# Half of the up projection with seven products per block instead of three eighths, and one of its weight sums formed by DMA

## The chip, the cores and the metric

The kernel runs on one core of one Trainium2 chip. What is measured is the device time of one launch in microseconds. Three timed runs of the kernel before gave 1578.73 to 1579.29 us, median 1578.91 us.

## The reference

One layer of an encoder: a retention branch and an attention branch, merged by gates, then an MLP with a squared ReLU. Batch 1, 256 tokens, width 2048, hidden width 8192, float32. Only the MLP matters for this change; `z` is what is tiled differently.

```python
def reference(x, positions, ...):
    h = x
    for l in range(DEPTH):
        u = _rmsnorm(h, norm_mix_g[l])
        h = h + _mixer(u, positions, ...)
        z = _rmsnorm(h, norm_mlp_g[l]) @ w_up[l]          # (256 x 2048) @ (2048 x 8192)
        h = h + jnp.square(jax.nn.relu(z)) @ w_down[l]    # (256 x 8192) @ (8192 x 2048)
    return _rmsnorm(h, norm_f_g)
```

## The kernel before

**Numbers as pairs.** Each float32 matrix is split in two parts, `hi` (rounded by ACT, line 550 in `split`, or 168) and `lo` (the rest, subtracted by DVE, line 551 or 169), and a product is formed as hi\*hi + hi\*lo + lo\*hi. So every weight tile is loaded by SP, cast by ACT, subtracted by DVE, and then used by PE.

**Two ways through the up projection.** The 8192 columns are cut into two kinds of work.

- A *unit* (class `Unit`) makes 128 columns for all 256 tokens. It has two parts, one for each half of the 16 blocks of depth; a part loads 512 KB (line 1225), splits it, and runs eight matmuls of 512 columns (line 176, hidden state hi and lo side by side) and eight of 256 columns (line 180). At its end ACT copies the sum out (1246), DVE adds the two halves (1247), ACT applies ReLU and square (1250, 1211), and POOL stores 128 KB of the hidden state to DRAM (1212).
- A *step* (class `Step`) multiplies 256 rows of depth by 1024 columns as 2x2 blocks with seven products in place of eight. A *group* is eight steps (j = 0 to 7), which accumulate seven PSUM tiles `zs`, one for each product; it makes 1024 columns, as many as eight units. A step has four parts: 0 (two products, from the loaded blocks `ra`), 1 (two, from the sum `fa`), 2 (two, from the sum `fb`), 3 (one, from the first block of `rb`). Each product is three matmuls of 512 columns (333 to 335).

Before the change three groups (`SU = 3`) make 3072 columns and 40 units the other 5120.

**A step's weights.** SP loads `ra` (two blocks, 512 KB, tile `sraw`, two buffers, line 300) and `rb` (two blocks, 512 KB, tile `raw`, five buffers which are shared with the units, line 301). DVE forms `fa` = `ra` + the second block of `rb` (line 307), and then `fb` = `fa` + blocks of `ra` and `rb` in two additions (316, 317). `fa` and `fb` lie in the tile `forms`, four slots used in turn, so those of a step are used again two steps later. `ra`, `fa`, `fb` and the first block of `rb` are then split, in that order, one for each part.

**End of a group.** When the last step of a group has run, `s_end` combines the seven PSUM tiles: four ACT copies (522 to 528) of products 3, 5, 1 and 7, and DVE additions (520), of which the first reads product 6, the second product 2, the third product 4. The seven tiles take all four banks of the pool `pmm` (products 3, 4, 2, 5) and three of the four of `pat` (6, 1, 7). The next group's tiles go into the same banks. A unit needs one bank of `pat`, and so does a *turn*: four transposes (1264) of the group's result, ReLU and square, and a store of 256 KB. Each group's four turns are spread over the steps 1 and later of the next.

**Order.** The order on ACT, DVE, PE, SP and POOL in the MLP is the program's own, written by `stream`: at part n it first issues the loads up to part n + 6, then the casts and subtractions up to part n + 4, then the matmuls of part n and, if that ends a unit, its copy out, then what is due later. There are seven pairs of buffers for `hi` and `lo` (four, and three named `more`). The list `parts` begins with three units (`EARLY`), then has the steps with units between them, then two units (`LATE`), and then the down projection, whose steps (`Seven`, a subclass of `Step`, and `Eight`) use the same loads and sums from `w_down`. Units are put after part 3 of every step but the last, and after part 1 of every second step.

Of the kernel before, what the change touches and what calls it, by code (L numbers as in the profile page):

```python
# [17 lines left out]
ALU = mybir.AluOpType  # L18

P = 128  # L20
# [7 lines left out]
CHUNK = 64  # L28
DFF = 8192
FT = DFF // P  # L30
SU = 3
SJ = KT // 2
ST = SU * 1024 // P
EARLY, LATE = 3, 2
AHEAD = 4
PAIRED = 6
MAKE = 7, 2 * EARLY + 18
SUMS = (4, 7, 10), (0, 1, 2)
MANUAL = {getattr(mybir.EngineType, n) for n in ('Activation', 'DVE', 'PE', 'SP', 'Pool')}
# [66 lines left out]
def block_kernel(ctx: ExitStack, tc: tile.TileContext, A):  # L106
    nc = tc.nc
    V, SC, G, PE = nc.vector, nc.scalar, nc.gpsimd, nc.tensor
# [7 lines left out]
    def big(name, dt=F32, shape=(P, KT, S)):  # L116
        return act.tile(list(shape), dt, tag="act16", name=name)

    class Pair:
        def __init__(self, name):  # L120
            self.t = [big(f"{name}{i}", F32R, (P, KT // 2, 2, S)) for i in range(2)]
# [35 lines left out]
    def wtile(kind, shape):  # L157
        uid[0] += 1
        dt, bufs = (F32, 5) if kind == "raw" else (F32R, 4)
        return wp.tile(shape, dt, tag=kind, bufs=bufs, name=f"{kind}{uid[0]}")  # L160

    def weights(src, shape, into=None):
        raw = wtile("raw", shape)
        hi, lo = into or (wtile(kind, shape) for kind in ("hi", "lo"))
        load = nc.sync.dma_start(raw, src)
        if uid[0] < 40:
            tc.keep_in_program_order(load)
        SC.copy(hi, raw)  # L168
        V.tensor_tensor(out=lo, in0=raw, in1=hi.bitcast(F32), op=ALU.subtract)  # L169
        return hi, lo  # L170
# [102 lines left out]
    def pair(shape):  # L273
        pool, more = env["pool"], env["more"]
        slot[0] += 1
        if slot[0] % (4 + more) < 4:
            return [wtile(kind, shape) for kind in ("hi", "lo")]
        if env["big"]:
            t = env["big"][:, slot[0] % (4 + more) - 4]
            n = math.prod(shape[1:])  # L280
            return [t[:, i, :n].rearrange("p (a b) -> p a b", a=shape[1]) for i in range(2)]
        return [
            pool.tile(shape, F32R, tag=f"more{kind}", bufs=more, name=f"more{kind}{uid[0]}_{slot[0]}")
            for kind in ("hi", "lo")
        ]

    class Step:
        def __init__(self, qs, src, x, j, between, end):
            self.qs, self.src, self.x, self.j, self.between, self.end = qs, src, x, j, between, end
            self.ws = {}  # L290

        def load(self, part):
            if part:
                return
            self.rb = wtile("raw", [P, 2, 512])
            if env["sraw"]:
                self.ra = env["pool"].tile([P, 2, 512], F32, tag="sraw", bufs=2, name=f"sraw{uid[0]}")
            else:
                self.ra = wtile("raw", [P, 2, 512])
            nc.sync.dma_start(self.ra, self.src[:, :2])  # L300
            nc.sync.dma_start(self.rb, self.src[:, 2:])
            forms = env["forms"]
            self.fa, self.fb = (forms[:, (2 * self.j + i) % forms.shape[1]] for i in range(2))

        def prep(self, part):
            if part == 0:
                V.tensor_tensor(  # L307
                    out=self.fa, in0=self.rb[:, 1:].to_broadcast([P, 2, 512]), in1=self.ra, op=ALU.add
                )
                self.middle()  # L310
            r = (self.ra, self.fa, self.fb, self.rb[:, :1])[part]
            hi, lo = pair([P, r.shape[1], 512])
            split(hi, lo, r)
            self.ws[part] = hi, lo
            if part == 0:
                V.tensor_tensor(out=self.fb[:, 0], in0=self.fa[:, 0], in1=self.ra[:, 1], op=ALU.add)
                V.tensor_tensor(out=self.fb[:, 1], in0=self.fb[:, 0], in1=self.rb[:, 0], op=ALU.add)
# [97 lines left out]
            pass  # L415

    class Seven(Step):
        def __init__(self, banks, src, h, n, end=None):
            super().__init__(None, src, None, n, None, end)
            self.banks, self.h = banks, h  # L420
# [127 lines left out]
    def split(hi, lo, val, scale=None):  # L548
        if scale is None:
            SC.copy(hi, val)  # L550
            V.tensor_tensor(out=lo, in0=val, in1=hi.bitcast(F32), op=ALU.subtract)  # L551
        else:
            SC.activation(hi, val, AF.Copy, scale=scale)
            V.scalar_tensor_tensor(
                lo, in0=val, scalar=scale, in1=hi.bitcast(F32), op0=ALU.mult, op1=ALU.subtract
            )
# [44 lines left out]
    for k in range(KT):  # L601
        t = lead0[:, N_VEC:] if k == 0 else wtile("raw", [P, LEAD])
# [654 lines left out]
    def turn(u, jj):  # L1257
        pT = atps(f"zt{u}{jj}")
        for j in range(2):
            kt = 2 * jj + j  # L1260
            for t in range(2):
                o = j * S + t * P
                src = zo[:, 0, 2 * t + kt // 4, kt % 4 * P : kt % 4 * P + P]
                PE.transpose(pT[:, o : o + P], src, ident)
        square(4 * u + jj, pT)

    def step(u, j, qs):
        def end():
            sums = s_end(qs, zo[:, 0].rearrange("p (t c) n -> p t c n", t=2), zo[:, 1])
            next(sums)  # L1270
            later.extend([d, lambda: next(sums)] for d in SUMS[u == SU - 1])
            turns.extend(lambda jj=jj: turn(u, jj) for jj in range(4))
# [13 lines left out]
    early = [Unit(i, 0) for i in range(EARLY)]  # L1286
    parts = [(e, h) for h in range(2) for e in early]
    units = list(range(EARLY, FT - ST - LATE))
    slots = [(u, j, h) for u in range(SU) for j in range(SJ) for h in (1, 3)][:-1]
    whole = [t for t in slots if t[2] == 3]  # L1290
    room = len(units) - len(whole)
    halves = [t for t in slots if t[2] == 1]
    if room >= 0:
        use = set(whole) | {halves[i * len(halves) // room] for i in range(room)}
    else:
        use = {t for t in whole if t[1] != PAIRED or t[0] >= -room}
    for u in range(SU):
        qs = {}
        for j in range(SJ):
# [69 lines left out]
    def finish(half, t, c, n, lo=0, hi=512):  # L1369
        h = residual(half, t, c)[:, lo:hi]  # L1370
        ps = both[half].q[ROLE[t, c]][:, lo:hi]
        V.scalar_tensor_tensor(h, in0=ps, scalar=rh2[:, t : t + 1], in1=h, op0=ALU.mult, op1=ALU.add)

        def square():
            SC.activation(ps, h, AF.Square, accum_out=ssf[:, t, n : n + 1])

        return square
# [90 lines left out]
    with tc.manual_schedule(engines=MANUAL):  # L1468
        stream(parts, after)
        assert not later  # L1470
        for t in range(2):
            for c in range(2):
# [10 lines left out]
                else:  # L1483
                    halves = [finish(1, t, 1, 3, 0, 256)]
# [86 lines left out]
```

## Time and profile before

| what | value |
|---|---|
| timed runs, median (lowest to highest) | 1578.91 us (1578.73 to 1579.29) |
| profiled execution, span from first to last instruction | 1577.3 us |
| mean granted TensorE clock | 0.998 |
| first product of the first step to the last of the last group | 907.9 to 1221.95 us |
| the second and the third group with its units | 107.05 us each |
| DMA in 905 to 1222 us | 69.80 MB, mean 220 GB/s |
| busy in the span: PE, DVE, ACT | 99%, 83%, 61% |

The profiled execution is described by its span; the median of the timed runs stands 1.6 us above it. PE's busy time is made of matmul records that overlap (a matmul of 512 columns has a record of 390 ns, and the next one begins some 0.23 us after it), so work on PE is read here from the starts of instructions, not from the sum of their durations. PEld is the loading of PE's weights, one in front of each matmul; its starts follow one another in the same rhythm. A row of the timeline that stands for several like instructions ends in x and their count.

### The profile page before, as it was taken

How to read it: one execution, taken by the hardware profiler on the slowest of the kernel's cores; microseconds unless marked ns; L12 is line 12 of the kernel's file. 1: busy time of each engine (PE TensorE's matmuls, PEld its weight loads, DVE VectorE, ACT ScalarE, POOL GpSimd, SP SyncE). 2: the span in 40 equal slices, each digit the busy share in tenths (PEclk: the TensorE clock that was granted, in tenths of full speed). 3: DMA queues.
4: the chain of work that ended last, by engine and by line, in shares of the span. 5: the costliest groups of instructions: out<-in, count | busy, mean ns of one | idle time of the engine just before them, and what ended most of it. 6: DMA issues, size and time to landing. Idle time of an engine off the chain costs nothing.

```text
span 1577.3 us, 21401 instructions
## 1 busy us (share of the span) xinstructions
PE 1565.2 (99%) x7671; PEld 1317.0 (84%) x7671; DVE 1313.6 (83%) x1780; ACT 959.0 (61%) x1405; POOL 38.9 (2%) x75
## 2 busy tenths in 40 slices
PE   9999999999999999999999999999999999999997
PEld 7888888888898888888888888888888888888886
DVE  7898877899967988875667689887978899989996
ACT  6545655566545667765445566676766766666664
POOL 0000000000000000000000000010000100000000
PEclk9999999999999999999999999999999999999999
DMA  8666655466656564443565666667675977786873
GB/s 322 212 197 205 231 164 161 157 203 208 204 178 222 190 203 142 136 135 132 188 214 186 240 221 226 218 209 236 203 246 196 366 267 244 241 308 216 267 254 114
DMA packets 107626, 333.70 MB, mean 212 GB/s; under 512 B 11264, under 2 KB 12160, under 8 KB 106496
## 3 DMA queue, kind: packets, MB, share of 16 engines
q1 hardware_dynamic: 104208, 318.71, 60.5%
q0 software_dynamic: 3168, 11.54, 1.8%
q10 hardware_dynamic: 144, 2.10, 0.4%
q8 instruction: 60, 0.98, 0.3%
q14 instruction: 46, 0.38, 0.1%
HBM read 319.72 MB, written 12.58 MB: 211 GB/s over the span
## 4 chain that ended last, share of the span: by engine, by line
PE 81%; issue 0%; DVE 0%; ACT 0%; DVEq 0%; POOLq 0%; POOL 0%; ACTq 0%
PE z L176 9%; PE dn L357 7%; PE dn L359 7%; PE dn L358 7%; PE z L180 5%; PE zs L333 2%; PE zs L334 2%; PE zs L335 2%; PE lt L199 2%; PE mo L214 2%; PE mo L217 2%; PE mo L215 2%; PE wo L214 2%; PE wo L215 2%; PE wo L217 2%; PE gm L357 2%
## 5 line engine op out<-in xcount | busy, mean ns | idle before, releaser
L169 DVE TENSOR_TENSOR lo<-raw,hi 128x1024 fp32r<-128x1024 f32 (+1 forms) x148 | 173.2, 1172 | 97.2 <-ACT hi L168 97.0
L551 DVE TENSOR_TENSOR lo<-raw,hi 128x1024 fp32r<-128x1024 f32 (+3 forms) x214 | 232.3, 1102 | 22.9 <-ACT hi L550 22.5
L168 ACT CAST hi<-raw 128x1024 fp32r<-128x1024 f32 (+1 forms) x148 | 149.4, 1011 | 166.2 <-PE mo L215 46.2
L550 ACT CAST hi<-raw 128x1024 fp32r<-128x1024 f32 (+3 forms) x214 | 200.1, 954 | 55.5 <-issue 7.8
L551 DVE TENSOR_TENSOR morelo<-raw,morehi 128x1024 fp32r<-128x1024 f32 (+1 forms) x118 | 127.2, 1099 | 19.6 <-ACT morehi L550 19.1
L550 ACT CAST morehi<-raw 128x1024 fp32r<-128x1024 f32 (+1 forms) x118 | 109.1, 950 | 12.6 <-DMA raw<-w_down 3.9
L550 ACT CAST hi<-forms 128x1024 fp32r<-128x1024 f32 x70 | 73.7, 1053 | 51.7 <-DVE forms L307 28.6
L176 PE MATMUL z<-hT,morehi 128*128 128x512 f32 x408 | 101.6, 391 | 0.0
L357 PE MATMUL dn<-hi,dd 128*128 128x512 f32 x230 | 89.7, 390 | 0.0
L359 PE MATMUL dn<-hi,dd 128*128 128x512 f32 x230 | 89.6, 390 | 0.0
L358 PE MATMUL dn<-lo,dd 128*128 128x512 f32 x230 | 89.6, 389 | 0.0
L551 DVE TENSOR_TENSOR lo<-forms,hi 128x1024 fp32r<-128x1024 f32 x70 | 85.0, 1221 | 5.3 <-ACT hi L550 4.9
L176 PEld LDWEIGHTS z<-hT,morehi 128*128 128x128 f32 x408 | 74.9, 188 | 14.4
L1246 ACT COPY hs<-z 128x512 f32<-128x512 f32 x40 | 23.5, 586 | 71.1 <-PE z L180 71.1
L358 PE MATMUL dn<-morelo,dd 128*128 128x512 f32 x156 | 60.8, 390 | 0.0
L357 PE MATMUL dn<-morehi,dd 128*128 128x512 f32 x156 | 60.8, 389 | 0.0
L359 PE MATMUL dn<-morehi,dd 128*128 128x512 f32 x156 | 60.8, 389 | 0.0
L180 PEld LDWEIGHTS z<-hT,morelo 128*128 128x128 f32 x408 | 55.7, 191 | 4.0
L176 PE MATMUL z<-hT,hi 128*128 128x512 f32 x232 | 57.9, 392 | 0.0
L307 DVE TENSOR_TENSOR forms<-raw,sraw 128x1024 f32<-128x1024 f32 x46 | 56.1, 1220 | 1.0 <-DMA raw<-w_up_s 1.0
L180 PE MATMUL z<-hT,morelo 128*128 128x256 f32 x408 | 56.9, 283 | 0.0
L214 PE MATMUL mo<-hi,my 128*128 128x512 f32 x128 | 50.8, 400 | 0.0
(498 smaller groups left out, 4193.8 us busy)
## 6 DMA issues: line engine op xcount, KB each, us to landing
raw<-w_down SPq DMA_DIRECT2D x106, 512.0 KB, 6.1
raw<-w_up SPq DMA_DIRECT2D x80, 512.0 KB, 5.1
raw<-w_rv SPq DMA_DIRECT2D x32, 512.0 KB, 4.8
raw<-w_rg SPq DMA_DIRECT2D x32, 512.0 KB, 4.2
raw<-w_gret SPq DMA_DIRECT2D x32, 512.0 KB, 4.6
raw<-w_ret_o SPq DMA_DIRECT2D x32, 512.0 KB, 5.1
raw<-w_gmla SPq DMA_DIRECT2D x32, 512.0 KB, 4.6
raw<-w_mla_o SPq DMA_DIRECT2D x32, 512.0 KB, 3.7
```

The source lines that it names most:

```text
L168: SC.copy(hi, raw)
L169: V.tensor_tensor(out=lo, in0=raw, in1=hi.bitcast(F32), op=ALU.subtract)
L176: PE.matmul(out, w[0][:, k], x.both(k0 + k), start=start and k == 0, stop=False)
L180: PE.matmul(out[:, :S], w[1][:, k], x.hi(k0 + k), start=False, stop=stop and k == n - 1)
L214: PE.matmul(out, x.hi(k0 + k, ts), w[0][:, k], start=start and k == 0, stop=False)
L215: PE.matmul(out, x.lo(k0 + k, ts), w[0][:, k], start=False, stop=False)
L217: PE.matmul(out, x.hi(k0 + k, ts), w[1][:, k], start=False, stop=stop and k == nk - 1)
L357: PE.matmul(q, ah, wh, start=start, stop=False)
L358: PE.matmul(q, ah, wl, start=False, stop=False)
L359: PE.matmul(q, al, wh, start=False, stop=self.left[f] == 0)
L550: SC.copy(hi, val)
L551: V.tensor_tensor(out=lo, in0=val, in1=hi.bitcast(F32), op=ALU.subtract)
```

## The change

`SU` is 4: four groups, 32 steps, make 4096 columns, and 32 units the other 4096. In the steps of the up projection (`added = True`) DVE's addition for `fa` is gone: SP loads the two blocks of `ra` a second time, from DRAM straight into `fa`, and POOL then issues a DMA that adds the second block of `rb`, read from DRAM and used for both halves, onto it. The steps of the down projection (`added = False`) form `fa` on DVE as before. The units are placed anew: one after part 3 of a step, spread evenly over 31 steps, so that 27 of these have one, and none after part 1.

```diff
-SU = 3
+SU = 4
...
-PAIRED = 6
...
     class Step:
+        added = True
+
...
             nc.sync.dma_start(self.rb, self.src[:, 2:])
             forms = env["forms"]
             self.fa, self.fb = (forms[:, (2 * self.j + i) % forms.shape[1]] for i in range(2))
+            if self.added:
+                nc.sync.dma_start(self.fa, self.src[:, :2])
+                G.dma_start(self.fa, self.src[:, 3:].to_broadcast([P, 2, 512]), accum_op=ALU.add)

         def prep(self, part):
             if part == 0:
-                V.tensor_tensor(
-                    out=self.fa, in0=self.rb[:, 1:].to_broadcast([P, 2, 512]), in1=self.ra, op=ALU.add
-                )
+                if not self.added:
+                    V.tensor_tensor(
+                        out=self.fa, in0=self.rb[:, 1:].to_broadcast([P, 2, 512]), in1=self.ra, op=ALU.add
+                    )
                 self.middle()
...
     class Seven(Step):
+        added = False
+
...
-    slots = [(u, j, h) for u in range(SU) for j in range(SJ) for h in (1, 3)][:-1]
-    whole = [t for t in slots if t[2] == 3]
-    room = len(units) - len(whole)
-    halves = [t for t in slots if t[2] == 1]
-    if room >= 0:
-        use = set(whole) | {halves[i * len(halves) // room] for i in range(room)}
-    else:
-        use = {t for t in whole if t[1] != PAIRED or t[0] >= -room}
+    whole = [(u, j, 3) for u in range(SU) for j in range(SJ)][:-1]
+    use = {whole[i * len(whole) // len(units)] for i in range(len(units))}
```

**PE, the border between the first and the second group, before.** `zs_8319` is product 7 of the first group; `zs_9314` and `zs_9315` are products 3 and 4 of the second, `zs_9316` is product 2; `z_9268` is a unit. Numbers behind the names are tile numbers.

```order
3664 L335 MATMUL zs_8319<-lo_9183,hT_7387 128x512
3665 L176 MATMUL z_9268<-hT_7386,morehi_60_9209 128x512 x8
3666 L180 MATMUL z_9268<-hT_7386,morelo_60_9210 128x256 x8
3667 L176 MATMUL z_9268<-hT_7387,morehi_61_9219 128x512 x8
3668 L180 MATMUL z_9268<-hT_7387,morelo_61_9220 128x256 x8
3669 L333 MATMUL zs_9314<-morehi_62_9235,hT_7386 128x512
```

The same border after the change; `zs_8324` is product 7 of the first group, `zs_9075`, `zs_9076` and `zs_9077` are products 3, 4 and 2 of the second.

```order
3648 L340 MATMUL zs_8324<-lo_8989,hT_7387 128x512
3649 L338 MATMUL zs_9075<-hi_9011,hT_7386 128x512
3650 L339 MATMUL zs_9075<-hi_9011,hT_7386 128x512
3651 L340 MATMUL zs_9075<-lo_9012,hT_7386 128x512
3652 L338 MATMUL zs_9076<-hi_9011,hc_7709 128x512
```

The unit that stood between the groups is gone there: steps 7, 15 and 23 in the count through all groups, the last of the first three, have none behind them, and step 30 has none either.

**SP, a stretch of the second half of the up projection, after the change.** `sraw` is `ra`, `raw` from `w_up_s` is `rb`, `forms` is the second load into `fa`, `raw` from `w_up` is a part of a unit.

```order
392 L306 DMA forms<-w_up_s 128x1024
393 L1232 DMA raw_9540<-w_up 128x1024
394 L1232 DMA raw_9563<-w_up 128x1024
395 L301 DMA sraw_9589<-w_up_s 128x1024
396 L302 DMA raw_9588<-w_up_s 128x1024
397 L306 DMA forms<-w_up_s 128x1024
```

Between the loads of two steps there are two unit parts (in places none) where there were four and two in turn, and each step has a third load of 512 KB, last of the three.

**POOL at the same border, after the change.** `hid` are the stores of the hidden state; before the change they were alone in this queue.

```order
40 L1219 DMA hid_8092<-hs_9008 128x256
41 L307 DMA forms<-w_up_s 128x2x512 x2
42 L1219 DMA hid_8072<-hs_9192 128x512
43 L1219 DMA hid_8093<-hs_9163 128x256
44 L307 DMA forms<-w_up_s 128x2x512
45 L1219 DMA hid_8073<-hs_9298 128x512
```

One adding DMA per step now stands in POOL's queue between the stores, each behind the stores issued earlier; two follow one another where no unit lies between two steps.

## The prediction

> **What bounds the kernel now.** I read first the table of windows, cut where the groups end (times from the span's start, then busy time and count of each engine, granted clock, DMA share, GB/s), then the chain of waits from 905 to 1230 us.
>
> ```profile
> core 0: us, PE busy (x) PEld busy (x) DVE busy (x) ACT busy (x) POOL busy (x), PEclk, DMA share, GB/s
> 1007.85:1114.90 107.05, 107.05 (x569) 92.13 (x568) 89.38 (x100) 73.05 (x104) 8.64 (x16) 1.00 0.66 221
> 1114.90:1221.95 107.05, 107.05 (x569) 92.15 (x568) 89.10 (x100) 73.44 (x105) 8.64 (x16) 1.00 0.66 219
> by line: PE z L176 41.6%; PE z L180 21.6%; PE zs L333 11.9%; PE zs L334 11.9%; PE zs L335 11.9%; PE zt L1264 1.2%; issue 0.0%
> PEld zs L335 <- DVE lo L551: 0.4, 1, 0.4
> ```
>
> In the up projection the chain is PE and nothing else, at full clock. The last row, from the list of waits of the same stretch, is the only wait of PE on data: 0.4 us. DVE is busy 83% of a group, ACT 68%, the DMA engines 66%. So what the change is worth is the time of PE's own rows, as long as the others keep up. PE's rhythm stands in the timeline of its weight loads.
>
> ```profile
> 1155.90 0.19 PEld L333 LDWEIGHTS zs<-hi,hc 128*128 128x128 f32 x1
> ...
> 1157.86 1.77 PEld L176 LDWEIGHTS z<-hT,morehi 128*128 128x128 f32 x8
> ...
> 1163.52 0.19 PEld L333 LDWEIGHTS zs<-hi,hT 128*128 128x128 f32 x1
> ...
> 1164.81 0.59 PEld L1264 LDWEIGHTS zt<-con,zo 128*128 128x128 f32 x4
> 1165.36 0.19 PEld L333 LDWEIGHTS zs<-hi,hc 128*128 128x128 f32 x1
> ...
> 1168.70 1.77 PEld L176 LDWEIGHTS z<-hT,morehi 128*128 128x128 f32 x8
> ```
>
> A unit takes 1163.52 - 1157.86 = 5.66 us. The step after it takes 5.18 us with a turn of 0.55 (1164.81 to 1165.36), so 4.63 us by itself; three products take 1157.86 - 1155.90 = 1.96 us, 0.65 each. A group checks it: 8 x 4.63 + 12 x 5.66 + 4 x 0.55 = 107.2 us, where the windows have 107.05.
>
> **Term 1, work on PE: -6.0 us.** Eight units go (-45.3 us), eight steps come (+37.0) with four turns (+2.2).
>
> **DVE gives up an addition and gets no freer.** Its rows in this stage:
>
> ```profile
> L551 DVE TENSOR_TENSOR lo<-forms,hi 128x1024 fp32r<-128x1024 f32 x48 | 58.1, 1221 | 4.9 <-ACT hi L550 4.9
> L307 DVE TENSOR_TENSOR forms<-raw,sraw 128x1024 f32<-128x1024 f32 x24 | 29.3, 1219 | 1.0 <-DMA raw<-w_up_s 1.0
> L1247 DVE TENSOR_TENSOR hs<-hs 128x256 f32<-128x256 f32 x40 | 17.0, 424 | 27.6 <-ACT hs L1246 26.6
> L317 DVE TENSOR_TENSOR forms<-forms,raw 128x512 f32<-128x512 f32 x24 | 16.6, 692 | 0.8
> L316 DVE TENSOR_TENSOR forms<-forms,sraw 128x512 f32<-128x512 f32 x24 | 16.5, 686 | 0.0
> 1002.54 0.69 DVE L551 TENSOR_TENSOR lo<-raw,hi 128x512 fp32r<-128x512 f32 x1
> ```
>
> A step without its first sum needs three subtractions of 1.22, one of 0.69 and fb's 0.69 + 0.69: 5.73 us; a unit needs 2 x 1.22 + 0.42 = 2.9. Over the stage: 24 x 1.22 = 29 us go with the additions and 8 x 2.9 = 23 with the units, 8 x 5.73 = 46 come with the steps and some 5.5 with a fourth end of a group (eight additions of 0.69). DVE keeps the same work in a shorter stage. That the addition is gone is worth nothing on PE's path by itself; it only makes room for the denser steps.
>
> **Term 2, the borders between groups: +8.7 us.** The even spread leaves no unit behind the last step of groups one to three. That unit covered the copying out of the seven PSUM tiles. The first four tiles of the next group need the four banks of products 3, 5, 2 and 4, in the order of their release: two ACT copies (lines 522, 524), then the second and the third DVE addition of line 520. Two borders in the timeline (PE's last product, ACT's copies, DVE's three additions):
>
> ```profile
> 1007.62 0.39 PE L335 MATMUL zs<-lo,hT 128*128 128x512 f32 x1
> 1007.85 1.98 PE L176 MATMUL z<-hT,morehi 128*128 128x512 f32 x8
> 1009.37 0.58 ACT L522 COPY zo<-zs 128x512 f32<-128x512 f32 x1
> 1009.85 0.59 ACT L524 COPY zo<-zs 128x512 f32<-128x512 f32 x1
> 1011.85 2.13 DVE L520 TENSOR_TENSOR zo<-zs,zo 128x512 f32<-128x512 f32 x3
> 1013.41 0.40 PE L333 MATMUL zs<-morehi,hT 128*128 128x512 f32 x1
> ...
> 1221.96 1.97 PE L176 MATMUL z<-hT,morehi 128*128 128x512 f32 x8
> 1223.87 2.13 DVE L520 TENSOR_TENSOR zo<-zs,zo 128x512 f32<-128x512 f32 x3
> ```
>
> The third addition ends 6.1 us after the group at the first border (1013.98 less 1007.85) and 4.0 us after it at the last. At the first, PE was in a unit until 1013.4, so it cost nothing. Without it the new group can run three products (1.96 us) and then waits with the fourth: 2.1 to 4.1 us a border. The order of DVE's queue gives a value between. ACT and DVE are let past the unit behind step 6 when PE ends it, 4.63 us before the group's end. Then come the copy out and the cast of the next ra (0.59 + 1.05), ra's subtraction 1.22, fb 1.38, two subtractions 2.44, one 0.69, the three additions 2.13: 9.5 us, so 4.9 after the end, less 1.96: 2.9 us. Three borders cost 8.7 us; bounds 6.3 to 12.3 from the two borders, and 2.3 if DVE had nothing left to do there (0.59 + 2.13 - 1.96 = 0.8 each).
>
> **Term 3, the way of the first sum through DMA: +6 us.** fa was formed by one addition of 1.22 us once ra and rb were there. Now it takes a load and then an adding DMA, one after the other, and behind it wait fb on DVE, the casts of fa and fb on ACT, the splits of all later parts, and, on ACT, the copies out of finished units. rb, and the second load of ra behind it on SP, wait for the fifth `raw` buffer back, that of the first part of the unit behind the step two earlier, which a DVE subtraction frees. From its start: the adding DMA lands after a time L; then DVE does fb (1.38), two subtractions (2.44), one (0.69), a unit's copy and addition (0.59 + 0.42), and the unit part that frees the buffer of the step two later (1.2 at most): some 6.3 us. A turn round this loop is two steps and two units, 2 x (4.63 + 5.66) = 20.6 us of PE. L may be 14.3 us. What it will be, from the list of DMAs in 905 to 1222 us (KB each, median us from issue to landing), the same list for 1140 to 1160 us, where the DMA share is 0.85, and the timeline of SP:
>
> ```profile
> DMA packets 19822, 69.80 MB, mean 220 GB/s; under 512 B 2641, under 2 KB 2641, under 8 KB 19799
> raw<-w_up_s SPq DMA_DIRECT2D x23, 512.0 KB, 4.3
> sraw<-w_up_s SPq DMA_DIRECT2D x22, 512.0 KB, 7.4
> hid<-hs POOLq DMA_DIRECT2D x38, 128.0 KB, 4.4
> hid<-hs POOLq DMA_DIRECT2D x8, 256.0 KB, 6.0
> ...
> q1 hardware_dynamic: 1283, 4.65, 75.0%
> q0 software_dynamic: 256, 0.79, 9.7%
> raw<-w_up SPq DMA_DIRECT2D x4, 512.0 KB, 6.9
> sraw<-w_up_s SPq DMA_DIRECT2D x2, 512.0 KB, 7.9
> ...
> 1046.58 0.33 SPq L301 DMA_DIRECT2D raw<-w_up_s  x1
> 1047.71 13.36 SPq L1225 DMA_DIRECT2D raw<-w_up  x4
> 1244.00:1248.00 4.00, 4.00 (x19) 3.34 (x18) 3.93 (x7) 1.88 (x3) 0.00 (x0) 1.00 1.07 440
> ```
>
> SP comes to its next load 1.1 us after rb's; the load lands in 4.3 to 7.9 us. No row shows an adding DMA. From below it is POOL's store of 256 KB, 6.0 us; from above it goes on as from 128 to 256 KB (1.6 us for each 128 KB): 9.2 us. L is between 11.4 and 18.2 us. I take 6.5 + 7.4 + 1.1 = 15.0: the load near `sraw`'s row, since it is last of a burst too, the adding DMA nearer to the store. That is 0.7 us over the 14.3, 0.35 a step, 9 us over the 27 steps that have a unit; the pauses at the borders let the queues catch up with a third. So +6, bounds 0 (L under 14.3) and 27 x 1.95 = 53.
>
> The DMA engines lean the same way. Eight steps and seven units load 19.9 MB and store 2.0 in 8 x 4.63 + 7 x 5.66 + 2.2 = 78.9 us: 277 GB/s where the windows had 220. The adding DMA writes 4.2 MB more: 331 GB/s; if it reads both its operands over the same path, 384, near the 440 of the busiest window quoted. The Trainium skill, page Collectives: The Full Stack, section "The bandwidth ceiling: the fold count and why AG ≠ RS ≠ AR", says that an adding transfer needs two source reads and so puts twice the traffic on the read side; by that the 384 holds, and the chance is with the last rival below. No row here shows it.
>
> **Sum.** -6.0 + 8.7 + 6 = +8.7 us on the profiled 1577.3: 1586.0. The median of the timed runs stands 1.6 us above that span: 1587.6, so 1588.
>
> **Rivals.**
>
> - *The borders alone.* L stays under 14.3 and DVE waits for no sum: 1578.9 - 6.0 + 8.7 = 1581.6. For it: the low rows, 1.1 + 4.3 + 6.0 = 11.4. Against it: these were taken at 220 GB/s. The Trainium skill, page DMA: Bandwidth & Descriptors, section "Anatomy of one DMA — SWDGE (gpsimd) path", gives 2.0 us plus the bytes at 436 GB/s for a DMA of POOL's, 3.2 us for 512 KB, by which this rival would hold; the trace disagrees, 4.4 us already for 128 KB.
> - *Faster.* PE's shorter work shows, since ACT and DVE arrive at the borders with nothing queued (0.8 us each, 2.3 in all) and the sums come in time: 1578.9 - 6.0 + 2.3 = 1575.2; with no pause at all, 1572.9. It decides if the third addition ends less than 3 us after a group. For it: PE never waits now, and DVE has 1.22 us less in front of these additions. Against it: both borders above, at 4.0 and 6.1 us.
> - *DMA or the loop as bound.* The adding DMA takes 9 us or more, or the engines fill up: L = 18, 0.5 x 3.7 x 27 = 50 us, partly over the borders' pauses: 1615 to 1630. For it: the 384 GB/s. Against it: loads queue no longer once the stage slows down.
> - *The change does not do what it says.* If the two DMAs were done early, long before the step, L would not matter. But the second load waits for rb's buffer in SP's queue. This is the first rival again.
>
> **Chances.** Forecast 0.45, borders alone 0.17, faster 0.17, DMA 0.21. 0.2% (3.2 us) is about what a measurement of this kernel tells from no change. Borders alone lies inside that by 0.5 us, so a part of it counts as slower and a part of the forecast's low edge as the same: faster 0.19, same 0.13, slower 0.68. The likeliest case alone reaches from 1582 to 1598. The range, with the faster case to 1574 and the DMA's to 1616: 1574 to 1616.
>
> **What would show it.** Term 1: a step of 4.63 and a unit of 5.66 us in PE's starts. Term 2: at three places a gap in PE between the third and the fourth product of a group, ended by line 520's DVE addition. Term 3: the issue list with a landing of some 7 us for the adding DMA; waits of DVE's fb on a DMA; PE waits after those of ACT's copies out. It is wrong if PE's starts have no gap at the borders, if the adding DMA lands in 4 us or in 10, or if the DMA share in the stage is over 0.95.

## The result, and the profile after

The changed kernel takes 1658.33 us, median of four runs (1656.46 to 1663.36), beside 1578.91 us (1578.73 to 1579.29) of the kernel before: ratio 1.0507, 95% interval 1.0491 to 1.0524. The forecast was 1588. The profiled execution has a span of 1661.3 us and a mean granted clock of 0.977.

From its page, the span and three rows of the 40 slices, each digit a tenth of a slice of 41.5 us:

```profile
span 1661.3 us, 21410 instructions
PE   9999999999999999999999789888988999999997
PEclk9999999999999999999999889999989999999999
DMA  9656655556475643435567788998889887776773
```

PE has gaps from the 23rd slice to the 31st, which is the stage with the steps, and the clock has an 8 in three of these. Before, that row of PE had a 9 in every slice but the last, and so had the clock in all. The row of DMA is fuller there but seldom full. The stage itself, first product of the first step to the last of the last group, in the table of windows (columns as in the prediction), and the chain of waits by line for 905 to 1305 us:

```profile
908.50:1304.70 396.20, 336.79 (x1584) 277.69 (x1583) 264.87 (x303) 222.04 (x308) 61.96 (x73) 0.91 0.86 255
by line: DMA forms<-w_up_s 49.2%; issue 8.9%; PE z L175 7.8%; PE zs L340 5.1%; PE zs L338 5.1%; PE zs L339 4.6%; PE z L179 4.3%; DVE lo L558 2.4%; ACT hi L557 2.3%; DVE forms L321 1.9%; DVE morelo L558 1.9%; ACT morehi L557 1.2%; DVE forms 
```

The stage takes 396.2 us where it took 314: 82 of the 84 us between the two profiled spans. PE is idle for 396.20 - 336.79 = 59.4 us of it, and the granted clock is 0.91 where it was 1.00. The chain, which was PE and nothing else before, is now for half of its time the two DMAs that write `forms`. Who waited for them, from the list of waits of 890 to 1320 us (total, times, longest), first the other engines, then PE's weight loads:

```profile
POOL forms L307 <- DMA forms<-w_up_s: 137.8, 21, 14.9
DVE forms L321 <- DMA forms<-w_up_s: 90.9, 19, 10.4
ACT hi L557 <- DMA forms<-w_up_s: 70.0, 15, 12.2
ACT morehi L557 <- DMA forms<-w_up_s: 55.5, 10, 11.8
...
PEld zt L1271 <- ACT hs L1253: 20.8, 5, 6.5
PEld zs L338 <- ACT zo L529: 15.5, 3, 7.6
PEld zs L338 <- ACT morehi L557: 14.2, 4, 8.8
```

POOL (line 307, the adding DMA) waits for the second load, DVE (321, `fb`) and ACT (557, the cast of `fa`) wait for the adding DMA, and PE waits for what stands behind that on ACT. None of PE's rows names a DMA: a wait two engines away reaches it as a late cast or a late copy. One step's first sum in the timeline (SP's load of `rb`, SP's second load into `fa`, POOL's adding DMA, DVE's first addition of `fb`):

```profile
1081.66 0.33 SPq L302 DMA_DIRECT2D raw<-w_up_s  x1
1082.08 0.51 SPq L306 DMA_DIRECT2D forms<-w_up_s  x1
1093.00 1.20 POOL L307 DMA_DIRECT2D forms<-w_up_s  x1 [10.03 <-DVE forms L322]
1103.10 0.69 DVE L321 TENSOR_TENSOR forms<-forms,sraw 128x512 f32<-128x512 f32 x1 [3.29 <-DMA forms<-w_up_s]
```

POOL's row names a DVE addition as what ended its wait, but the slot in `forms` was free when SP issued the second load into it at 1082.08, so it is that load that POOL waits for; the list above has it so in 21 cases. From the load of `rb` to `fb` it is 21.4 us, 11.3 until POOL issues and 10.1 from there. Over the 32 steps (the first from 887.60 to 902.84, the last from 1276.22 to 1298.89) the mean is 18.8 us: 9.5 and 9.2. The prediction had 7.6 and 7.4 in these places. In 19 of the 32 steps DVE's `fb` waits for the adding DMA, and these have the same mean of 18.8 us. The list of DMAs in 905 to 1305 us:

```profile
DMA packets 32639, 102.57 MB, mean 256 GB/s; under 512 B 3589, under 2 KB 3589, under 8 KB 32613
q1 hardware_dynamic: 21776, 78.90, 57.9%
q0 software_dynamic: 10832, 23.34, 27.7%
forms<-w_up_s POOLq DMA_DIRECT2D x31, 512.0 KB, 8.7
forms<-w_up_s SPq DMA_DIRECT2D x30, 512.0 KB, 8.1
```

The second load lands in 8.1 us (assumed: 6.5) and the adding DMA in 8.7 (assumed: 7.4), while the DMA engines are 86% busy.

What a late sum does to the clock stands in one pause: the last product before it, DVE's and ACT's first work behind the sum, PE's next products, and then four windows of 4 us.

```profile
931.35 0.39 PE L340 MATMUL zs<-morelo,hc 128*128 128x512 f32 x1
938.72 0.69 DVE L321 TENSOR_TENSOR forms<-forms,sraw 128x512 f32<-128x512 f32 x1 [10.29 <-DMA forms<-w_up_s]
940.15 0.80 PE L338 MATMUL zs<-morehi,hc 128*128 128x512 f32 x1 [8.41 <-ACT morehi L557]
947.75 0.63 PE L340 MATMUL zs<-lo,hT 128*128 128x512 f32 x1
928.00:932.00 4.00, 3.74 (x21) 2.89 (x19) 0.43 (x1) 0.00 (x0) 1.84 (x2) 1.00 1.02 400
936.00:940.00 4.00, 0.00 (x0) 0.00 (x0) 1.24 (x2) 0.94 (x1) 1.19 (x1) 0.50 0.78 159
944.00:948.00 4.00, 4.00 (x11) 3.14 (x10) 4.00 (x6) 2.89 (x5) 0.58 (x1) 0.50 0.71 195
948.00:952.00 4.00, 4.00 (x22) 3.39 (x22) 3.93 (x5) 1.57 (x2) 0.00 (x0) 0.96 0.92 331
```

PE stands still for 8.4 us. The clock is then 0.50, and stays there for about 8 us after PE has work again: a product's record is 0.63 us long instead of 0.39, and in 4 us 11 matmuls start instead of 22. A busy PE at half clock is hard to see in shares of busy time; the count of matmuls and the clock's column show it.

### The profile page after: what moved, and what is told of

Its sections match the earlier page's. It is cut to its first block, busy times and chain, and to the rows that moved or that the text cites. A ratio compares the mean times of both kernels' runs of the same rounds, so it can differ in the third digit from the quotient of the medians.

```text
span 1661.3 us, 21410 instructions
## 1 busy us (share of the span) xinstructions
PE 1589.7 (96%) x7599; PEld 1326.0 (80%) x7599; DVE 1313.7 (79%) x1787; ACT 967.5 (58%) x1409; POOL 77.1 (5%) x103
## 4 chain that ended last, share of the span: by engine, by line
PE 64%; DMA 12%; issue 3%; DVE 2%; ACT 1%; POOL 0%; SPq 0%; DVEq 0%; POOLq 0%; ACTq 0%
DMA forms<-w_up_s 12%; PE dn L364 7%; PE dn L363 7%; PE dn L362 7%; PE z L175 3%; PE lt L198 2%; PE mo L213 2%; PE mo L216 2%; PE mo L214 2%; PE wo L213 2%; PE wo L214 2%; PE wo L216 2%; PE gm L362 2%; PE yr L363 2%; PE yr L362 2%
## 5 line engine op out<-in xcount | busy, mean ns | idle before, releaser
L558 DVE TENSOR_TENSOR lo<-raw,hi 128x1024 fp32r<-128x1024 f32 (+3 forms) x236 | 252.8, 1085 | 31.0 <-ACT hi L557 30.3
L321 DVE TENSOR_TENSOR forms<-forms,sraw 128x512 f32<-128x512 f32 x54 | 37.1, 688 | 91.0 <-DMA forms<-w_up_s 90.9
L557 ACT CAST morehi<-forms 128x1024 fp32r<-128x1024 f32 x50 | 52.6, 1051 | 92.8 <-DMA forms<-w_up_s 55.5
L558 DVE TENSOR_TENSOR morelo<-raw,morehi 128x1024 fp32r<-128x1024 f32 (+1 forms) x88 | 93.3, 1080 | 4.3 <-ACT morehi L557 4.3
L557 ACT CAST morehi<-raw 128x1024 fp32r<-128x1024 f32 (+1 forms) x88 | 80.7, 936 | 6.4 <-DMA raw<-w_down 2.4
L307 POOL DMA_DIRECT2D forms<-w_up_s x32 | 39.2, 1224 | 613.9 <-PE ht L1186 393.2
L175 PEld LDWEIGHTS z<-hT,hi 128*128 128x128 f32 x296 | 54.4, 189 | 10.6
L558 DVE TENSOR_TENSOR morelo<-forms,morehi 128x1024 fp32r<-128x1024 f32 x50 | 60.9, 1221 | 1.2 <-ACT morehi L557 0.6
L175 PE MATMUL z<-hT,morehi 128*128 128x512 f32 x216 | 53.8, 391 | 0.0
L363 PEld LDWEIGHTS dn<-lo,dd 128*128 128x128 f32 x240 | 45.1, 188 | 9.4
```

Source lines behind the costliest of these rows:

```text
L175: PE.matmul(out, w[0][:, k], x.both(k0 + k), start=start and k == 0, stop=False)
L307: G.dma_start(self.fa, self.src[:, 3:].to_broadcast([P, 2, 512]), accum_op=ALU.add)
L363: PE.matmul(q, ah, wl, start=False, stop=False)
```

## Experiments

All times are medians beside runs of the kernel before in the same session, which had medians of 1578.4 to 1578.7. "Idle" is the stage's time less PE's busy time in it.

| run | what | us | ratio (95%) | stage, idle (us) |
|---|---|---|---|---|
| e1_dve | `fa` by DVE in all steps | 1586.18 | 1.0047 (1.0032 to 1.0062) | 320.7, 8.4 |
| e2_dve_cover | e1, borders covered by units | 1581.41 | 1.0019 (1.0009 to 1.0029) | 315.3, 4.2 |
| e3_dma_cover | the change, borders covered | 1672.60 | 1.0595 (1.0571 to 1.0618) | 402.5, 65.0 |
| e5_no_acc | second load, no adding DMA | 1582.35 | 1.0021 (1.0010 to 1.0031) | 316.6, 6.1 |
| e8_plain_pool | one plain DMA of POOL's for both | 1582.09 | 1.0021 (1.0010 to 1.0031) | |
| e7_early | both DMAs a step earlier | 1590.36 | 1.0074 (1.0054 to 1.0094) | 322.7, 8.9 |
| e9_early_cover | e7, borders covered | 1587.38 | 1.0059 (1.0038 to 1.0079) | 322.1, 7.8 |
| e10_half | e9, adding DMA in odd steps only | 1579.45 | 1.0004 (0.9995 to 1.0013) | 312.8, 2.3 |
| e14_half_even | e10 with the even steps | 1582.22 | 1.0024 (1.0014 to 1.0033) | |
| e11_half_front | e10, ten units in the first group | 1584.83 | 1.0037 (1.0024 to 1.0050) | |
| e4_su3_dma | the kernel before, its sums by the two DMAs | 1653.74 | 1.0473 (1.0454 to 1.0493) | 388.0, 51.1 |
| e12_su3_early | e4, both DMAs a step earlier | 1579.24 | 1.0006 (0.9997 to 1.0016) | 314.5, 0.0 |
| p_short | the kernel before, 12 short pauses of PE | 1635.35 | 1.0358 (1.0338 to 1.0379) | |
| p_long | the kernel before, 3 long pauses | 1614.70 | 1.0228 (1.0207 to 1.0248) | |

None beats the kernel before; e10 and e12 can't be told from it.

**e1: the additions back on DVE, the rest of the change kept.**

```diff
-        added = True
+        added = False
```

> The change with the first sum formed on DVE again; 32 steps and the new places of the units stay. Theory A (the loop: second load and adding DMA take some 18 us one after the other, behind a buffer that frees late; PE pauses, and after a pause its granted clock is halved for some us): without the two DMAs only the pauses at the three borders are left, 1578 to 1592 us. Rival B (the DMA engines are full): the same 1578 to 1592, since their work falls by a quarter. Rival C (the places of the units and the denser steps make most of the loss): above 1610 us.

The kernel loses 7.5 us instead of 79: the two DMAs make 72 of the loss, and the rest of the change the other 7.5. It is still slower than the kernel before, and DVE is busy for 298.48 us of a stage of 320.7.

**e2 and e3: units kept behind the last step of each group, and left out behind the seventh.** e2 has the sums on DVE, e3 by DMA.

```diff
-    use = {whole[i * len(whole) // len(units)] for i in range(len(units))}
+    use = {t for t in whole if t[1] != 6}
```

> As e1, and the units are placed so that each group's last step has one behind it (the steps without one are j = 6 of each group). My term 2 says that e1 less this is 8.7 us (2.3 to 12.3): 1573 us if DVE keeps up with the denser steps, 1580 to 1590 if it does not. If the borders cost nothing, e1 and this agree within 2 us.

> The change as it is (second load and adding DMA), with the units placed as in e2. Theories A and B: the borders are a small part, 1640 to 1658 us. Rival C: under 1610 us.

Covered borders are worth 4.8 us with the sums on DVE, and the time is then in the range that was given for a DVE that does not keep up (1580 to 1590). With the sums by DMA they cost 14 us more, where a gain was expected: a miss. PE's waits for ACT's copies at the borders (15.5 us in the change) are gone in e3, but its waits in a turn grew from 20.8 us, and those for ACT's casts into `morehi` from 14.2, to these (list of waits of e3):

```profile
PEld zt L1271 <- ACT hs L1253: 29.7, 6, 8.0
PEld zs L338 <- ACT morehi L557: 20.2, 4, 9.0
```

PE still waits behind the same late sums (DVE and ACT wait for the two DMAs for 240.5 us in all, 216.4 in the change): the pauses moved to other places, since the borders had not been their cause. Why they grew is not shown.

**e5: the second load stays, the adding DMA goes** (the first sum lacks the block of `rb`).

```diff
                 nc.sync.dma_start(self.fa, self.src[:, :2])
-                G.dma_start(self.fa, self.src[:, 3:].to_broadcast([P, 2, 512]), accum_op=ALU.add)
```

> The change with the adding DMA left out and the second load kept: fa is ra alone, so the products that use fa and fb do not have the added block. Theory A: L falls from 18 us to the load's 7 to 8 and is under the 14.3 us that the loop allows; only the borders are left, 1580 to 1592 us. Rival: if the second load alone (its bytes, its place in SP's queue) makes the loss, above 1620 us.

Its stage, PE's three waits at the second border with DVE's three additions of the group's end between them, and `rb`'s load and the first addition of `fb` of one step:

```profile
907.50:1224.10 316.60, 310.51 (x1585) 262.56 (x1584) 265.84 (x303) 222.21 (x308) 22.96 (x42) 1.00 0.78 267
1068.19 0.19 PEld L337 LDWEIGHTS zs<-hi,hT 128*128 128x128 f32 x1 [1.93 <-ACT zo L528]
1068.92 2.13 DVE L526 TENSOR_TENSOR zo<-zs,zo 128x512 f32<-128x512 f32 x3
1070.38 0.19 PEld L337 LDWEIGHTS zs<-hi,hc 128*128 128x128 f32 x1 [0.95 <-DVE zo L526]
1071.11 0.19 PEld L337 LDWEIGHTS zs<-hi,hc 128*128 128x128 f32 x1 [0.20 <-DVE zo L526]
1022.41 0.33 SPq L302 DMA_DIRECT2D raw<-w_up_s  x1
1036.94 0.69 DVE L320 TENSOR_TENSOR forms<-forms,sraw 128x512 f32<-128x512 f32 x1
```

This is the change with its PE program whole and no late sum. The stage of 316.6 us is about what the first two terms make: before's 313.95 less 6.0, plus 8.7, is 316.65 (the last product starts 0.2 us behind the window's end, so half a us is open). The gaps of a border are 1.93 + 0.95 + 0.20 = 3.1 us, and the clock stays at 1.00. The last two rows give the time that a sum may take here: `fb` comes 14.5 us after `rb`'s load, which is also the median of the 32 steps (5.3 to 16.9). The changed kernel's loss over this run is 396.2 - 316.6 = 79.6 us of stage, and it comes with the adding DMA, which has to wait for the second load: 59.4 - 6.1 = 53.3 us more of idle PE, and 336.79 - 310.51 = 26.3 us more of busy PE for the same products. Most of the latter is half clock: in windows of 1 us over the stage, the busy time times the missing part of the clock adds up to 24 us, and to nothing in e5.

**e8: one plain DMA of POOL's in place of the two** (again without the block of `rb`).

```diff
-                nc.sync.dma_start(self.fa, self.src[:, :2])
-                G.dma_start(self.fa, self.src[:, 3:].to_broadcast([P, 2, 512]), accum_op=ALU.add)
+                G.dma_start(self.fa, self.src[:, :2])
```

> The change with one plain DMA from POOL in the place of both: it copies the two blocks of ra into fa, 512 KB, adds nothing (the products that use fa and fb lack the added block). It shows what of the adding DMA's 8.7 us comes from POOL's queue and what from the adding. If it lands in 5 to 6 us the adding costs some 3 us; if in 8 us, the queue does. The time: no loop, so 1580 to 1592 us.

POOL's queue in its list of DMAs, 905 to 1230 us:

```profile
q0 software_dynamic: 6864, 23.34, 20.0%
forms<-w_up_s POOLq DMA_DIRECT2D x31, 512.0 KB, 6.4
```

No loss over e5: a DMA of POOL's in each step is not the cost by itself. The same 23.34 MB written take 20.0% of 325 us of the engines, 65 us, where the adding DMAs took 27.7% of 400 us, 111 us. The stores alone are 17.9 us (5.5% of 325 in e5). An adding DMA of 512 KB so takes (111 - 17.9) / 31 = 3.0 us of all 16 engines, a plain one (65 - 17.9) / 31 = 1.5. It lands 2.3 us later, 8.7 us for 6.4, in a stage with a DMA share of 0.86 for 0.78.

**e7 and e9: the same two DMAs, a step earlier.** They are issued with the loads of part 2 of the step before, and no longer wait behind `rb` in SP's queue. e9 also has the units of e2.

```diff
+        def first(self):
+            fa = env["forms"][:, 2 * self.j % env["forms"].shape[1]]
+            nc.sync.dma_start(fa, self.src[:, :2])
+            G.dma_start(fa, self.src[:, 3:].to_broadcast([P, 2, 512]), accum_op=ALU.add)
...
+            if part == 2 and self.follow:
+                self.follow.first()
...
-            if self.added:
-                nc.sync.dma_start(self.fa, self.src[:, :2])
-                G.dma_start(self.fa, self.src[:, 3:].to_broadcast([P, 2, 512]), accum_op=ALU.add)
+            if self.added and not self.ahead:
+                self.first()
```

> The change, with second load and adding DMA of a step issued where the third part of the step before it is loaded, ahead of that step's units on SP and POOL, so that they no longer wait for rb's buffer; the same bytes and the same DMAs. Theory A: the loop is cut, pauses shrink to the borders and a few others, 1580 to 1610 us. Rival B: the stage cannot be shorter than the work of its DMA engines (342 us of 16 engines by the trace of the change, against 317 us of the stage before), 1604 to 1650 us. If the time stays within 10 us of 1658, the place of the second load does not matter at all.

> Second load and adding DMA early as in e7, and the units placed as in e2, with one behind each group's last step. Theory A: e7's 1590.4 us less the borders (e1 less e2 was 4.8 us, e7's profile has some 16 us of PE waits on the copies at the borders): 1574 to 1584 us. Rival B (engines full: e7 has a DMA share of 1.0 over the stage): the time stays at 1587 to 1594, since PE then waits elsewhere.

e7's stage and its DMA queues in 905 to 1230 us:

```profile
909.10:1231.80 322.70, 313.83 (x1584) 264.80 (x1583) 264.87 (x302) 221.38 (x307) 60.62 (x72) 0.99 1.00 313
q1 hardware_dynamic: 21594, 78.37, 65.8%
q0 software_dynamic: 10763, 23.21, 33.7%
```

Sixty-eight of the 79 us come back with the same DMAs and the same bytes (102 MB). So it is the moment of issue that counts, not the traffic. DVE and ACT still wait for the two DMAs, 37.1 us in place of 216.4. The engines are now full, 65.8 + 33.7%; that this is the next bound is likely but not shown. Covering the borders gains 3.0 us here, less than the spread of e9's runs (1584.68 to 1592.95).

**e10, e14 and e11: half of the sums by DMA.** Early issue and covered borders as in e9; `st.added = j % 2 == 1`, in e14 `== 0`; e11 is e10 with ten units in the first group in place of seven.

> As e9, but only every second step forms its first sum by DMA, the others on DVE: the DMA work falls by some 45 us of 16 engines, DVE gets 20 us more than in e9 and 20 less than in e2. If DVE bounds e2 (59.5 us of 60 busy there) and the DMA engines bound e9, this is the fastest of the three, 1572 to 1577 us, and faster than the kernel before. If PE's own rows are the bound in e9 already, it agrees with e9 within 2 us.

> As e10, but the steps with even j form the first sum by DMA, so that the first step of each group, where DVE also has the additions of the group before, is relieved. If the short waits on DVE behind the borders are what keeps e10 from PE's own 1573 us: 1573 to 1577.5 us, faster than the kernel before. If it makes no difference which half: 1578 to 1581 us.

> As e10, with ten units in the first group, where DVE also makes the last combinations of the hidden state and where most of PE's short waits on DVE were (three of the four over 0.3 us), six in the second and third, five in the fourth; each border between groups is covered. If DVE's load in the first group is what keeps e10 from PE's own 1573 us: 1573 to 1577 us. If not, or if the later groups now wait as much: 1578 to 1582 us.

With half of the adding DMAs the engines are 85% busy and DVE 280.6 us of 312.8, and DVE and ACT wait for the two DMAs for only 12.3 us, but the gain stops at the kernel before: the six us of PE's work that were the prize are spent in small waits, 5.5 us of PE's weight loads for DVE. The even steps in place of the odd (e14) are 2.8 us slower, so relieving the first step of a group does not help. More units in the first group made it worse: PE's weight loads then wait for DVE's splits (line 566) 13 times, 8.9 us in all, where e10 has 5 times and 4.2 us.

**e4 and e12: the two DMAs alone, in the kernel before** (three groups, 24 steps, its own places of units); e12 issues them as e7 does.

> The kernel before (three groups, its own places of the units) with the second load and the adding DMA in its 24 steps, issued as in the change. Theory A: on average a turn of the loop here is two steps and three units, 2 x 4.63 + 3 x 5.66 = 26.2 us, so L may be 19.9 us, more than the 17 to 18 us measured; few pauses, 1578 to 1590 us. If the two DMAs cost the same at any density (for each step what the change lost, 88 us over 32), it is 1640 us.

> e4 (three groups, the kernel before's places of the units, the two DMAs in each of 24 steps) with second load and adding DMA issued where the third part of the step before is loaded. Theory A, with the lead taken step by step instead of on average: in e4 every second step has rb's buffer free only 12 us before its sum is due, and the two DMAs took 17.6 us there; issued earlier they are hidden, 1576 to 1588 us. If the two DMAs cost a fixed time per step wherever they are issued, it stays at 1640 to 1655 us.

e4 was a miss. I took the mean: a turn of the loop is longer there (26.9 us of PE for two steps and three units), so a sum of 15 to 20 us had room. The timeline shows two kinds of steps. First the kernel before, two steps: their loads of `rb` and their first additions of `fb`, behind the addition of the step ahead.

```profile
1063.30 0.68 DVE L316 TENSOR_TENSOR forms<-forms,sraw 128x512 f32<-128x512 f32 x1
1067.01 0.33 SPq L301 DMA_DIRECT2D raw<-w_up_s  x1
1073.83 0.33 SPq L301 DMA_DIRECT2D raw<-w_up_s  x1
1079.64 0.69 DVE L316 TENSOR_TENSOR forms<-forms,sraw 128x512 f32<-128x512 f32 x1
1090.15 0.68 DVE L316 TENSOR_TENSOR forms<-forms,sraw 128x512 f32<-128x512 f32 x1
```

The lead is 12.6 us in the one step and 16.3 in the next. Behind a step with two units the fifth `raw` buffer back is that step's own `rb`, so the next `rb` comes 3.7 us after its `fb`. The same kind of step in e4:

```profile
1015.31 0.69 DVE L322 TENSOR_TENSOR forms<-forms,sraw 128x512 f32<-128x512 f32 x1 [1.30 <-DMA forms<-w_up_s]
1019.03 0.33 SPq L303 DMA_DIRECT2D raw<-w_up_s  x1
1025.93 1.23 POOL L308 DMA_DIRECT2D forms<-w_up_s  x1 [3.71 <-DMA forms<-w_up_s]
1036.67 0.69 DVE L322 TENSOR_TENSOR forms<-forms,sraw 128x512 f32<-128x512 f32 x1 [8.63 <-DMA forms<-w_up_s]
```

Again 3.7 us to `rb`, but then 17.6 to the next `fb`: 21.4 in place of 16.3, and that step is late by 5 us. e12 takes nothing away but the lateness, at a DMA share of 0.95, and loses nothing: at this density the DMAs have no fixed cost that could be measured.

**p_short and p_long: what a pause of PE costs.** In the kernel before, two transposes with a chain of ACT copies between them: 1 + 3 copies at four steps of a group, 1 + 24 at one.

```diff
+    def pause(n):
...
+        PE.transpose(ps[:, :P], ident, ident)
+        SC.copy(d[:, :P], ps[:, :P])
+        for _ in range(n):
+            SC.copy(d[:, :P], d[:, :P])
...
+        PE.transpose(ps[:, :P], d[:, :P], ident)
...
```

> The kernel before with twelve short pauses of PE (two transposes with a copy of the first and three more copies on ACT between them, at j = 1, 3, 4 and 6 of each group), of some 1.5 to 2.5 us each by ACT's rows. Clock theory: no pause reaches the length at which the granted clock falls; it stays at 0.99 or more, and the time is 1578.9 plus the pauses themselves, 1597 to 1609 us.

> The kernel before with three long pauses of PE of the same kind (24 more copies on ACT, at j = 3 of each group), of some 6 to 9 us each, about the same sum as p_short. Clock theory: after each the clock is halved for some 3 to 7 us, so the time is 1578.9 plus the pauses plus 2 to 4 us each; the granted clock of the stage falls. Rival: a pause costs its own length, long or short, and the change's slow matmuls come from something else.

p_short's stage, a window ahead of one of its pauses, the end of the pause and a window behind it, and one pause of p_long:

```profile
890.00:1300.00 410.00, 376.55 (x1898) 318.32 (x1897) 295.62 (x338) 257.80 (x411) 29.15 (x54) 0.95 0.58 195
956.00:958.00 2.00, 2.00 (x10) 1.39 (x8) 2.00 (x4) 2.00 (x3) 0.00 (x0) 1.00 0.07 14
960.59 0.33 PE L526 MATMUL gap977b<-con,idle 128*128 128x128 f32 x1 [2.57 <-ACT idle L524]
962.00:964.00 2.00, 2.00 (x6) 1.52 (x6) 1.97 (x3) 1.65 (x3) 0.00 (x0) 0.50 0.93 375
```

```profile
962.22 0.47 PE L526 MATMUL gap976b<-con,idle 128*128 128x128 f32 x1 [9.49 <-ACT idle L524]
960.00:964.00 4.00, 1.78 (x5) 1.49 (x6) 0.02 (x1) 3.25 (x10) 0.00 (x0) 0.50 0.02 6
964.00:968.00 4.00, 4.00 (x17) 3.23 (x17) 4.00 (x4) 2.78 (x3) 0.00 (x0) 0.84 0.45 91
```

I expected that short pauses leave the clock alone; most do not. A pause of 2.57 us is followed by a window at 0.50, in which 6 matmuls start in 2 us where 10 did. The twelve waits of PE behind ACT's copies are 3.51 us (once), 3.18 (four times), 2.57 (once) and 1.77 (six times, each shortly behind another wait of 0.68). The clock went to 0.50 at ten of them, and stayed at 1.00 at two of 1.77 us. e1's borders show the same on both sides: PE's wait of 2.39 us at the first was followed by 0.50, those of 2.03 us at the other two by 1.00. So no one length decides in these runs, and what does is open.

In p_short PE idles for 410 - 376.55 = 33.5 us, and the kernel loses 57: some 20 us go beyond the idle time and the 24 transposes (0.14 us each, 3.4 us by my estimate), 1.7 us a pause. p_long loses 36.3 us, of which 29.7 are idle PE and 0.8 its six transposes by the same estimate: 1.9 us a pause beyond its length, less than the 2 to 4 expected. The Trainium skill, page TensorE: Matmul & The Clock Gate, section "HAM oscillation — how this bites in real kernels", gives the rule that PE should have no idle gaps over some 3.4 us. The trace agrees for the long pauses; of the eleven waits of 1.77 to 3.18 us in p_short nine differ from it, and the measurement decides.

## Why the prediction was wrong

The direction and the place were right; the time was outside the range because one term of the sum was mis-sized and one price was missing.

**Term 1, PE's work (-6.0), held.** Term 2, the borders (+8.7), held too: e5 contains both and nothing else, and its stage is the predicted sum within half a us; its time, 1582.35, is near that of the rival "borders alone" (1581.6). The inside of term 2 was not quite as told. The larger part of the gap lies ahead of the first product and is ended by an ACT copy, not between the third and the fourth and ended by DVE. The size came out because the gap's end is where the prediction put it: the fourth product starts at 1071.11, right behind the third addition (1068.92 + 2.13), which ends 4.5 us after the group where 4.9 was forecast. At which product PE waits before that makes no difference.

**Term 3, the way of the first sum through DMA (+6), is the step that failed.** Its loop was right: 14.3 us allowed, a median of 14.5 in e5. Its L was not. "6.5 + 7.4 + 1.1 = 15.0" stands against a mean of 18.8, above the upper bound of 18.2 as well. In the same order the means are 8.9 from the second load to POOL's issue, 9.2 from there to `fb`, and 0.7 between SP's two loads. The second load landed in 8.1 us for 6.5, POOL issued some 0.8 us after that, which had no number at all, and the adding DMA landed in 8.7 for 7.4. The prices leaned on rows at 220 GB/s, and the term that they belonged to raises the traffic (255 GB/s in the stage). A small excess over 14.3 is multiplied by 27 steps: with 18.8 the term's own formula gives (18.8 - 14.3) / 2 x 27 = 61 us, near the 53.3 us of idle PE. The prediction chose L within a us of the threshold, and so made the sum depend on the one number that it knew worst.

**The clock is the price that was missing.** All pauses were priced at their length. In the changed kernel 26.3 us of the 79.6 are busy PE beyond e5's for the same products, most of it half clock behind pauses, and p_short and p_long show that a pause costs 1.7 to 1.9 us more than it lasts, on average. How much of the 26 would go if the clock stayed at full is open: PE waits for the loop anyway, and faster products would in part only wait longer.

**The rivals.** "DMA or the loop as bound" (1615 to 1630) named the mechanism, the loop, and missed the size by the same two errors. Its other half, full engines, did not decide here (share 0.86); e7 and e9 reach a share of 1.00, and whether it bounds them is not shown. "The change does not do what it says" was right in its remark that the second load waits for `rb`'s buffer; e7, where the two DMAs are issued a step earlier and no longer stand behind `rb`, is 68 us faster, much the largest single piece. The remark was read as a reason to dismiss the rival, when, with the adding DMA behind it, it was the reason for the loss (e5 keeps this wait without that DMA and loses nothing beyond the borders). "Faster" fell with the borders; e10, with the borders covered and half of the sums early, shows that the 6 us of term 1 do not come out even then.

**The doubled read side.** The prediction cited the Trainium skill, page Collectives: The Full Stack, section "The bandwidth ceiling: the fold count and why AG ≠ RS ≠ AR", for two source reads per adding transfer. The trace fits it: 3.0 us of the engines against 1.5 for the plain DMA of the same size (e8). It does not single it out: the adding DMA also moves its bytes in more packets, 272 against 144 (the queue's counts less e5's 2400 for the stores, over 31), and its source is one block used twice, in rows half as long. No run separates the two. The other rule that it cited from the Trainium skill, page DMA: Bandwidth & Descriptors, section "Anatomy of one DMA — SWDGE (gpsimd) path", 3.2 us for a DMA of 512 KB of POOL's, does not hold beside this kernel's traffic: 6.4 us plain (e8) and 8.7 adding.

## What to carry to other kernels

A sum that moves from an engine to DMA moves from a throughput to a latency: read in the trace of before how long its first consumer comes after the load that the sum stands behind, in every kind of step and not in the mean, and compare that with the whole way (load, issue, adding DMA), priced at the traffic of after. If the two lie within a few us, issue the DMAs a step earlier before judging the idea; here that was 68 of 79 us. In this kernel a pause of PE of some 2 us or more cost nearly 2 us on top for the clock, in most cases; a price for pauses needs that term.

## What the runs showed of the hardware

An adding DMA of 512 KB took 3.0 us of all 16 engines and landed in 8.7 us, a plain one from the same queue 1.5 and 6.4. The granted clock went to 0.50 at ten of p_short's twelve pauses of PE, among them waits of 1.77 us behind one of 0.68, and stayed at 1.00 at the other two and at two waits of 2.03 us in e1. The borders of e5, split in gaps of 1.93, 0.95 and 0.20 us with products between, left it at 1.00. DMA engines carried 313 GB/s at a share of 1.00 in e7, below the 331 to 384 that the prediction had asked of them, without slowing PE by more than some 6 us (stage 322.7 beside 316.6 in e5).
